# Output rows 0 to 3 projected in two parts, the sparse features before the differential ones

## The chip, the core and the metric

The kernel runs on one core of a Trainium2 chip. The core has five engines with an instruction stream each: TensorE (PE in the profile; its weight loads are PEld), VectorE (DVE), ScalarE (ACT), GpSimd (POOL) and SyncE (SP), which issues nearly all transfers here. An engine takes its instructions in order and waits on semaphores for the others. The metric is the device time of one execution in microseconds (us).

## The reference

One decoder layer on 1024 tokens of width 1024, in float32. `h = x @ w_in` gives queries, keys, values and gates. Two groups of heads share it. The differential group (4 heads of 128 features) computes two causal softmaxes per head, subtracts one from the other, multiplies by the values and normalizes each row. The sparse group (8 heads of 64) adds a compressed, a selected and a window attention. Then:

```python
mix = jnp.concatenate([o_diff, o_nsa], axis=-1) @ w_out[l]
x = layer_norm(DEEPNORM_ALPHA * x + mix, ln1_g[l], ln1_b[l])
ffn = (jax.nn.silu(x @ w_gate[l]) * (x @ w_up[l])) @ w_down[l]
x = layer_norm(DEEPNORM_ALPHA * x + ffn, ln2_g[l], ln2_b[l])
```

So 512 of the 1024 features that `w_out` multiplies are differential (k = 0 to 3 in pieces of 128, one piece a head) and 512 are sparse (k = 4 to 7).

## The kernel before

The 1024 tokens are 8 rows of 128. A product in near float32 is made of three matmuls (`mm3`, L116 to L118): each operand is split into a high part, a cast on ScalarE (L81), and a low part, a subtraction on VectorE or GpSimd (L83); high x high, high x low and low x high are summed in one bank of PSUM. There are eight banks: two named psS (scores), three psT (transposes), one psO (attention times values) and two psM (projections).

Attention goes by units. A unit of a differential head is one row of 128 queries. Its front half makes the scores (L323, L326) in pieces of up to 512 keys, adds distances and takes the minimum on VectorE (L332), and takes the exponentials on ScalarE (L346); its back half transposes the weights (L355) and multiplies by the values (L481). When four rows of a head are through (rows 0 to 3 or 4 to 7), `finish` normalizes them (L495 on VectorE, L496 on GpSimd, L497 on VectorE), transposes them (L500, the tile `od`), scales them on ScalarE (L503) and stores them to DRAM, into `mix_d` (L505). The sparse heads store theirs there too, all of them before the last four phases.

What happens between the units is set by a table, `phases`. A row of it names units and a list of fillers: generators that issue the projections of the next heads, and at the end the output projection. A function `pump` draws from the list at a rate that the fillers' stated costs and the units' costs give, and gives what it draws a lower priority. The final order on each engine is then made by a scheduler from these priorities; the order listings below show what it made.

The output projection of row i (`out_fill` for rows 0 to 3, `out_start` and `out_half_now` for rows 4 to 7): x of the row is loaded to `acc[i]`, the mixed features of the row are loaded from `mix_d` into two `w` tiles of which there are five (the sparse half first, then the differential), and for each half of the output's columns 8 pieces k, in the order 4 to 7 and then 0 to 3, are summed in one bank; then `acc = ALPHA * acc + bank` on VectorE (L605). The `w_out` weights lie in eight tiles of the pool `big`, which has eight; they replace the tiles of `x` (four for tokens 0 to 511, four for 512 to 1023) once no projection reads these. `norm1` is the layer norm of a row (L633, L645 to L648, L655) and its store. After the attention, `x_put` transposes the normalized rows (L913) and `x_sums` forms sums of rows i and i-4 (L929 to L934) for the gate and up products, whose first matmul reads `x11h`.

A row's differential half has all four differential heads in it, so its load waits until head 3's half (rows 0 to 3, or 4 to 7) is stored.

Of the kernel before, what the change touches and what calls it, by code (L numbers as in the profile page):

```python
# [17 lines left out]
P = 128  # L18
# [19 lines left out]
def layer_kernel(ctx: ExitStack, tc: tile.TileContext, xT, x, w_t, w_vg, w_dv, lam_in, subln,  # L38
# [21 lines left out]
    def ps_m():  # L60
        return psum.tile([P, 512], F32, tag="M", name="psM", bufs=2)
# [31 lines left out]

    def load_split_here(src, hi, lo, l_eng="dve", order=(0,)):

        n = 1024 // len(order)
        for k in order:
            raw = lo[:, k * n:(k + 1) * n].bitcast(F32)
            nc.sync.dma_start(raw, src[:, k * n:(k + 1) * n])
            split(raw, hi[:, k * n:(k + 1) * n], lo[:, k * n:(k + 1) * n], l_eng)  # L100
        return hi, lo

    def w_tiles():
        lo = w_tile()
        return w_tile(), lo
# [4 lines left out]
    def big_tiles():  # L110
        t = big_tile()
        return [t[:, 0, :], t[:, 1, :]]

    def mm3(acc, ah, al, bh, bl, first, last, more=False):

        nc.tensor.matmul(acc, lhsT=ah, rhs=bh, start=first, stop=False, skip_group_check=more)  # L116
        nc.tensor.matmul(acc, lhsT=ah, rhs=bl, start=False, stop=False, skip_group_check=more)  # L117
        nc.tensor.matmul(acc, lhsT=al, rhs=bh, start=False, stop=last, skip_group_check=more)  # L118
# [25 lines left out]
    with ExitStack() as ctx_a:  # L144
# [294 lines left out]

            return [make(i, kind) for i in range(NB) for kind in range(2)]  # L440

        late = []

        def diff_units(h, qt, kd, V):
            slope = SLOPES[h]
# [2 lines left out]
            def make(i):  # L448
# [42 lines left out]
                def finish(orow, ss, r0):  # L491

                    nc.vector.tensor_mul(r0, r0, r0)
                    nc.vector.tensor_scalar(r0, r0, EPS, None, op0=ALU.mult)
                    nc.vector.scalar_tensor_tensor(ss, ss, 1.0 / P, r0, op0=ALU.mult, op1=ALU.add)  # L495
                    nc.gpsimd.tensor_tensor(ss, ss, mhalf[:, :4], op=ALU.pow)  # L496
                    nc.vector.tensor_mul(orow, orow, ss.unsqueeze(2).to_broadcast([P, 4, P]))  # L497
                    tp = ps_t()
                    for n in range(4):
                        nc.tensor.transpose(tp[:, n * P:(n + 1) * P], orow[:, n, :], ident)  # L500
                    for n in range(2):
                        md = small([P, 256], "tmp", 3)
                        nc.scalar.activation(md, tp[:, n * 256:(n + 1) * 256], AF.Copy, scale=g08)  # L503
                        b = hf * 4 + n * 2
                        nc.sync.dma_start(mix_d[b:b + 2, :, h, :].rearrange("i p t -> p i t"),  # L505
                                          md.rearrange("p (i t) -> p i t", t=P))

                return front, back, 2.0 * (i + 1) + 1

# [67 lines left out]
                    yield 0.0  # L577
            return steps, 0.0

        def wo_fill(nh):  # L580
            def steps():
                for kp in range(KT // 2):
                    wo[nh, kp] = load_split_here(wo_d[nh, kp], *big_tiles(), l_eng="pool", order=(0, 1))
                yield 0.0
            return steps, 0.0

        mix_rows = {}

        def out_start(i):

            acc[i] = slot((8, 9, 10, 11, 4, 2, 3, 5)[i], F32)
            nc.sync.dma_start(acc[i], x[i * P:(i + 1) * P, :])
            mix_rows[i] = load_split_here(mix_d[i].rearrange("p k t -> p (k t)"), *w_tiles(),
                                           "dve" if i < 4 else "pool", order=(1, 0))

        def out_half(i, nh, ps):
            m = mix_rows[i]
            cs = slice(nh * 512, (nh + 1) * 512)
            for k in (4, 5, 6, 7, 0, 1, 2, 3):
                ks = slice(k * P, (k + 1) * P)  # L600
                ws = slice((k % 2) * 512, (k % 2 + 1) * 512)
                w = wo[nh, k // 2]
                mm3(ps, m[0][:, ks], m[1][:, ks], w[0][:, ws], w[1][:, ws], k == 4, k == 3)
                yield 0.65
            nc.vector.scalar_tensor_tensor(acc[i][:, cs], acc[i][:, cs], ALPHA, ps, op0=ALU.mult, op1=ALU.add)  # L605

        def norm1(i, **kw):
            layer_norm(acc[i], **kw)
            nc.sync.dma_start(x1_d[i], acc[i])

        def out_fill(i, normed):
            def steps():
                out_start(i)
                for nh in range(2):
                    yield from out_half(i, nh, ps_m())
                if normed:
                    norm1(i)
            return steps, 10.4

        def norm_params(src, after=None):  # L620
            lnp[:] = [slot(0, F32), slot(1, F32)]
# [156 lines left out]
        def qdf(h, hf, tiles=w_tiles):  # L778
            return q_fill(8 + 2 * h, hf, qd[h], tiles)
# [14 lines left out]
        def held_fill():  # L794

            def steps():
# [23 lines left out]
            ([(diff, 2, range(4))],  # L820
             [kdf(3, 0), kdf(3, 1), qdf(3, 0)], 2, 1.25, 130, None),
            ([(diff, 3, range(4))],
             [qdf(2, 1), dvf(1, range(4, 8))], 2, 1.25, 60, None),
            ([(diff, 2, (4, 7, 6, 5))],
             [wo_fill(0), qdf(3, 1), wo_fill(1), held_fill(), out_fill(0, False), out_fill(1, False)], 2, 1.25, 40, None),
            ([(diff, 3, range(4, 8))],
             [ln_fill((0, 1)), out_fill(2, True), out_fill(3, True)], 2, 0.9, 60, None),
        ]
        pending = []

# [103 lines left out]
        nc.gpsimd.tensor_sub(b21, b21, t2)  # L934

    def out_half_now(i, nh, ps):
        for _ in out_half(i, nh, ps):
            pass

    for i in (4, 5):  # L940
        out_start(i)
# [329 lines left out]
```

## Time and profile before

| what | us |
| --- | --- |
| median of 3 runs (lowest, highest) | 1305.22 (1305.02, 1305.49) |
| the profiled execution, its time | 1305.84 |
| its span, first to last instruction | 1304.1 |
| TensorE busy | 1286.2 (99%) |
| VectorE busy | 917.8 (70%) |
| ScalarE busy | 652.1 (50%) |
| GpSimd busy | 464.1 (36%) |
| mean granted TensorE clock | 0.999 |

A row of the timeline gives the start and the duration in us, the engine, the line of the kernel, the operation, out<-in with the tiles' names, the shape and how many; behind it, in brackets, the engine's idle time before it and what ended it. A matmul's duration overlaps the next one's, so how long one takes in a stream is read from start to start.

### The profile page before, as it was taken

Reading aid. Unit: us, or ns where it says so; the run is one execution under the profiler, and the core shown is the slowest. Engines: PE = TensorE matmul, PEld = TensorE weight load, DVE = VectorE, ACT = ScalarE, POOL = GpSimd, SP = SyncE. Lnnn points to the kernel's source line nnn. Section 1 sums busy time; section 2 is a strip of 40 time slices with the busy share of each in tenths; the row PEclk is TensorE's granted clock in tenths of the full one; section 3 lists DMA queues with packets and bytes.
Section 4 is the critical chain, followed back from the end, with each engine's and each line's share of the span. In section 5 each row is a group of like instructions: output and inputs, shape, how many; then the busy total and the mean of one; then the engine's idle time right before and its main releaser. Section 6 shows DMA issues by size and latency. Waiting matters only on the chain.

```text
span 1304.1 us, 20490 instructions
## 1 busy us (share of the span) xinstructions
PE 1286.2 (99%) x6955; PEld 1107.8 (85%) x6955; DVE 917.8 (70%) x1963; ACT 652.1 (50%) x1398; POOL 464.1 (36%) x499
## 2 busy tenths in 40 slices
PE   9999999999999999999999999999999999999997
PEld 7998999988988889788887888888888888888886
DVE  5567867778778667774797677776766768555588
ACT  5366866868776566653353333333333335533330
POOL 4434534545435446643613313232231222000071
PEclk9999999999999999999999999999999999999999
DMA  9412012121112135623224566555555559768641
GB/s 354 132 31 62 22 35 62 49 48 48 35 55 70 50 94 149 218 82 113 81 76 149 180 232 228 194 178 173 174 170 185 187 179 346 259 200 291 195 168 65
DMA packets 86841, 183.13 MB, mean 140 GB/s; under 512 B 10576, under 2 KB 19152, under 8 KB 86608
## 3 DMA queue, kind: packets, MB, share of 16 engines
q1 hardware_dynamic: 86736, 181.82, 42.7%
q8 instruction: 55, 0.90, 0.3%
q14 instruction: 50, 0.41, 0.1%
HBM read 116.18 MB, written 57.15 MB: 133 GB/s over the span
## 4 chain that ended last, share of the span: by engine, by line
PE 91%; DVE 4%; DMA 2%; ACT 2%; issue 1%; POOL 0%; SPq 0%; DVEq 0%; ACTq 0%
PE psM L116 11%; PE psM L118 11%; PE psM L117 11%; PE psS L118 6%; PE psS L117 6%; PE psS L116 6%; PE psT L118 5%; PE psT L117 5%; PE psT L116 5%; PE psT L365 4%; PE psS L323 3%; PE psS L326 3%; PE psO L428 2%; PE psO L426 2%; PE psO L481 2%; PE psO L116 2%
## 5 line engine op out<-in xcount | busy, mean ns | idle before, releaser
L346 ACT ACTIVATE t<-t,m 128x384 f32<-128x384 f32 (+7 forms) x192 | 144.2, 752 | 65.4 <-DVE m L332 59.8
L411 POOL TENSOR_SCALAR t<-t,r,gates 128x640 f32<-128x640 f32 (+7 forms) x128 | 99.6, 783 | 180.5 <-DVE r L405 82.4
L116 PE MATMUL psM<-big,w 128*128 128x512 f32 x304 | 120.6, 397 | 0.6 <-DVE slot L171 0.3
L118 PE MATMUL psM<-big,w 128*128 128x512 f32 x304 | 120.1, 396 | 0.0
L117 PE MATMUL psM<-big,w 128*128 128x512 f32 x304 | 119.9, 394 | 0.0
L323 PE MATMUL psS<-slot,q 128*128 128x320 f32 (+10 forms) x304 | 111.8, 369 | 2.2 <-DVE m L332 2.0
L1019 POOL TENSOR_TENSOR half<-half,half 128x512 f32<-128x512 f32 x22 | 33.5, 1524 | 205.0 <-ACT half L1018 205.0
L83 DVE TENSOR_TENSOR pt<-psT,pt 128x512 fp32r<-128x512 f32 (+1 forms) x152 | 91.3, 615 | 13.1 <-ACT pt L81 11.7
L326 PE MATMUL psS<-slot,q 128*128 128x320 f32 (+10 forms) x304 | 99.5, 329 | 0.0
L81 ACT CAST pt<-psT 128x512 fp32r<-128x512 f32 (+1 forms) x152 | 77.3, 525 | 20.6 <-PE psT L365 10.0
L81 ACT CAST big<-slot 128x1024 fp32r<-128x1024 f32 (+1 forms) x54 | 54.4, 1018 | 66.2 <-DVE slot L1011 50.5
L83 DVE TENSOR_TENSOR op<-op 128x1024 fp32r<-128x1024 f32 x44 | 60.9, 1388 | 36.3 <-ACT op L81 35.8
L83 DVE TENSOR_TENSOR big<-slot,big 128x1024 fp32r<-128x1024 f32 (+1 forms) x54 | 63.5, 1182 | 30.5 <-ACT big L81 30.3
L365 PE MATMUL psT<-ident,t 128*128 128x128 f32 x528 | 83.8, 273 | 0.8 <-DVE pt L83 0.7
L81 ACT CAST op<-op 128x1024 fp32r<-128x1024 f32 x44 | 45.9, 1052 | 61.8 <-DMA op<-t_d 55.6
L428 PE MATMUL psO<-pt,slot 128*128 128x256 f32 x264 | 72.1, 294 | 0.1
L426 PE MATMUL psO<-pt,slot 128*128 128x256 f32 x264 | 71.8, 289 | 0.0
L332 DVE CUSTOM_DVE_ANT_0 t<-psS,dsel 128x384 f32<-128x384 f32 (+9 forms) x128 | 62.3, 493 | 13.4 <-PE psS L326 9.6
L1023 POOL TENSOR_TENSOR half<-half,half 128x512 f32<-128x512 f32 x22 | 36.5, 1659 | 99.0 <-DVE half L1022 98.8
L81 ACT CAST big<-big 128x1024 fp32r<-128x1024 f32 (+1 forms) x49 | 44.2, 912 | 45.6 <-DMA big<-t_d 34.0
L118 PEld LDWEIGHTS psM<-big,w 128*128 128x128 f32 x304 | 57.1, 188 | 11.4
L116 PEld LDWEIGHTS psM<-big,w 128*128 128x128 f32 x304 | 57.2, 188 | 11.1 <-ACT w L81 0.8
(371 smaller groups left out, 3971.3 us busy)
## 6 DMA issues: line engine op xcount, KB each, us to landing
a_d<-slot SPq DMA_DIRECT2D x77, 256.0 KB, 3.0
t_d<-slot SPq DMA_DIRECT2D x77, 256.0 KB, 2.2
q<-q SPq DMA_DIRECT2D x48, 256.0 KB, 2.9
slot<-in_w_up_dram SPq DMA_DIRECT2D x22, 512.0 KB, 3.8
slot<-in_w_down_dram SPq DMA_DIRECT2D x22, 512.0 KB, 3.9
op<-a_d SPq DMA_DIRECT2D x44, 256.0 KB, 3.5
op<-t_d SPq DMA_DIRECT2D x44, 256.0 KB, 4.0
big<-a_d SPq DMA_DIRECT2D x33, 256.0 KB, 2.9
```

Of the source, the lines that this page charges most:

```text
L81: nc.scalar.copy(hi, src)
L83: eng.tensor_sub(lo, src, hi.bitcast(F32))
L116: nc.tensor.matmul(acc, lhsT=ah, rhs=bh, start=first, stop=False, skip_group_check=more)
L117: nc.tensor.matmul(acc, lhsT=ah, rhs=bl, start=False, stop=False, skip_group_check=more)
L118: nc.tensor.matmul(acc, lhsT=al, rhs=bh, start=False, stop=last, skip_group_check=more)
L323: mm = nc.tensor.matmul(ps[:, :c + part], lhsT=q[0], rhs=k[:, ks], start=True, stop=False)
L326: nc.tensor.matmul(ps[:, :c + part], lhsT=q[1], rhs=k[:, ks], start=False, stop=True)
L346: nc.scalar.activation(t[:, :width], t[:, :width], AF.Exp, bias=m, scale=-1.0, accum_out=r)
L365: nc.tensor.transpose(tp[:rows, n * P:(n + 1) * P], s, ident)
L411: nc.gpsimd.tensor_scalar(t, t, r[:, c:c + 1], gates[:, i, gc:gc + 1], op0=ALU.mult, op1=ALU.mult)
L426: nc.tensor.matmul(po[:, :256], lhsT=v, rhs=pt[:, 0, n * 256:(n + 1) * 256], start=False, stop=False)
L428: nc.tensor.matmul(po[:, :256], lhsT=v, rhs=pt[:, 1, n * 256:(n + 1) * 256], start=False, stop=last)
```

## The change

Rows 0 to 3 of the output are projected in two parts. A part is half of the features (four pieces k) for both halves of the columns; it loads its half of the mixed row into one `w` tile, high and low beside each other, and is put down by itself. The sparse part (part 1) loads x of the row and does `acc = ALPHA * acc + bank`; the differential part (part 0) does `acc = acc + bank`. The sparse parts of rows 0 to 3 stand as fillers from the phase of head 3's rows 0 to 3 on; the differential parts behind `held_fill` and in the last phase. The weights are loaded for the sparse pieces of both column halves first (`wo_fill((2, 3))`), and for the differential ones later. Rows 4 to 7 keep their form.

```diff
-        def wo_fill(nh):
+        def wo_fill(kps):
             def steps():
-                for kp in range(KT // 2):
-                    wo[nh, kp] = load_split_here(wo_d[nh, kp], *big_tiles(), l_eng="pool", order=(0, 1))
+                for nh in range(2):
+                    for kp in kps:
+                        wo[nh, kp] = load_split_here(wo_d[nh, kp], *big_tiles(), l_eng="pool", order=(0, 1))
...
+        def out_mm(nh, ps, m, ks, k, first, last):
+            w, ws = wo[nh, k // 2], slice((k % 2) * 512, (k % 2 + 1) * 512)
+            mm3(ps, m[0][:, ks], m[1][:, ks], w[0][:, ws], w[1][:, ws], first, last)
...
-        def out_fill(i, normed):
+        def out_fill(i, part, normed=False):
             def steps():
-                out_start(i)
+                if part:
+                    row_start(i)
+                t = w_tile()
+                m = t[:, 0:512], t[:, 512:1024]
+                src = mix_d[i].rearrange("p k t -> p (k t)") if part else mix_row(i)
+                load_split_here(src[:, part * 512:(part + 1) * 512], *m, "dve")
                 for nh in range(2):
-                    yield from out_half(i, nh, ps_m())
+                    ps, cs = ps_m(), slice(nh * 512, (nh + 1) * 512)
+                    for k in range(4):
+                        out_mm(nh, ps, m, slice(k * P, (k + 1) * P), 4 * part + k, k == 0, k == 3)
+                        yield 0.65
+                    if part:
+                        nc.vector.scalar_tensor_tensor(acc[i][:, cs], acc[i][:, cs], ALPHA, ps,
+                                                       op0=ALU.mult, op1=ALU.add)
+                    else:
+                        nc.vector.tensor_add(acc[i][:, cs], acc[i][:, cs], ps)
                 if normed:
                     norm1(i)
-            return steps, 10.4
+            return steps, 5.2
...
             ([(diff, 3, range(4))],
-             [qdf(2, 1), dvf(1, range(4, 8))], 2, 1.25, 60, None),
+             [wo_fill((2, 3)), qdf(2, 1), dvf(1, range(4, 8)), out_fill(0, 1)], 2, 1.25, 60, None),
             ([(diff, 2, (4, 7, 6, 5))],
-             [wo_fill(0), qdf(3, 1), wo_fill(1), held_fill(), out_fill(0, False), out_fill(1, False)], 2, 1.25, 40, None),
+             [out_fill(1, 1), qdf(3, 1), wo_fill((0, 1)), out_fill(2, 1), out_fill(3, 1), held_fill(), out_fill(0, 0)],
+             2, 1.25, 40, None),
             ([(diff, 3, range(4, 8))],
-             [ln_fill((0, 1)), out_fill(2, True), out_fill(3, True)], 2, 0.9, 60, None),
+             [ln_fill((0,)), out_fill(1, 0, True), out_fill(2, 0, True), out_fill(3, 0, True)], 2, 0.9, 60, None),
```

The new functions `row_start` (the load of x) and `mix_row` (the row in DRAM) are pieces of the old `out_start`. In the listings line numbers of the change are higher by some 20 than the same line's before: L913 and L935 are the transposes of `x_put`, L605 and L613 the old addition of a half row, L648 and L669 the last addition of a layer norm, L929 and L951 the first of `x_sums`.

First place: TensorE, shortly ahead of the transposes of head 3's first half (`od_6708`), while head 2's last scores (128x384) and products with the values (psO) are made. Before:

```order
L326 MATMUL psS_7178<-slot0_6049,q_6786 128x384
L481 MATMUL psO_6973<-slot6_5637,pt_6979 128x128 x4
L323 MATMUL psS_7183<-slot1_6050,q_6787 128x384
L326 MATMUL psS_7183<-slot1_6050,q_6787 128x384
L323 MATMUL psS_7188<-slot1_6050,q_6787 128x384
L326 MATMUL psS_7188<-slot1_6050,q_6787 128x384
L481 MATMUL psO_7019<-slot6_5637,pt_7025 128x128 x4
L323 MATMUL psS_7327<-slot2_6467,q_7084 128x320
```

And with the change:

```order
L117 MATMUL psM_7303<-big_6723,w_7299 128x512
L481 MATMUL psO_7035<-slot6_5637,pt_7041 128x128 x4
L323 MATMUL psS_7181<-slot1_6050,q_6770 128x384
L326 MATMUL psS_7181<-slot1_6050,q_6770 128x384
L323 MATMUL psS_7186<-slot1_6050,q_6770 128x384
L326 MATMUL psS_7186<-slot1_6050,q_6770 128x384
L118 MATMUL psM_7303<-big_6723,w_7299 128x512
L116 MATMUL psM_7317<-big_6730,w_7299 128x512
```

The rows psM belong to the sparse part of row 3 (`w_7299`, weights `big`); twelve of psM_7317 follow before the next L481, where before no projection stood. From the transposes of head 2's first half to these of head 3's, 72 matmuls with 512 columns of projection and output stand now, 18 before.

Second place: TensorE at the transposes of head 3's second half. Before (`od_7456`; psM_7683 is row 3's second half of the columns, of which 22 matmuls and three more groups of transposes follow until psS_7857, row 4's first differential piece):

```order
L117 MATMUL psM_7683<-big_7105,w_7647 128x512
L500 MATMUL psT_7776<-ident_74,od_7456 128x128 x4
L913 MATMUL psT_7815<-ident_74,slot8_7135 128x128 x4
L913 MATMUL psT_7822<-ident_74,slot8_7135 128x128 x4
L118 MATMUL psM_7683<-big_7105,w_7646 128x512
L116 MATMUL psM_7683<-big_7105,w_7647 128x512
```

And with the change (psS_7873 and psS_7899 are row 4's two banks, `w_7814` the high part of its mixed row):

```order
L118 MATMUL psM_7981<-big_6737,w_7823 128x512
L500 MATMUL psT_7792<-ident_74,od_7500 128x128 x4
L935 MATMUL psT_7831<-ident_74,slot8_6929 128x128 x4
L935 MATMUL psT_7838<-ident_74,slot8_6929 128x128 x4
L935 MATMUL psT_7845<-ident_74,slot9_7093 128x128 x4
L935 MATMUL psT_7852<-ident_74,slot9_7093 128x128 x4
L935 MATMUL psT_7859<-ident_74,slot10_7252 128x128 x4
L116 MATMUL psS_7873<-big_7224,w_7814 128x512
L117 MATMUL psS_7873<-big_7224,w_7814 128x512
```

The transposes of rows 0 to 2 now stand together between head 3's transposes and row 4's first differential piece, and no output matmul with them.

Third place: VectorE at row 6 (`slot3`) and row 7 (`slot5`). Before:

```order
L648 TENSOR_TENSOR slot3_8023<-slot3_8023,slot1_7471 128x1024
L929 TENSOR_TENSOR slot10_7498<-slot3_8023,slot10_7498 128x512
L930 TENSOR_TENSOR half0_8179<-slot3_8023 128x512
L932 TENSOR_TENSOR half1_8180<-slot3_8023,slot10_7498 128x512
L605 SCALAR_TENSOR_TENSOR slot5_8033<-slot5_8033,psM_8153 128x512
L655 BN_STATS st_8199<-slot5_8033 128x6
L633 BN_AGGR mv_8202<-st_8199 128x2
```

And with the change:

```order
L613 SCALAR_TENSOR_TENSOR slot5_8049<-slot5_8049,psM_8169 128x512
L676 BN_STATS st_8215<-slot5_8049 128x6
L669 TENSOR_TENSOR slot3_8039<-slot3_8039,slot1_7515 128x1024
L654 BN_AGGR mv_8218<-st_8215 128x2
L951 TENSOR_TENSOR slot10_7252<-slot3_8039,slot10_7252 128x512
L952 TENSOR_TENSOR half0_8195<-slot3_8039 128x512
L129 TENSOR_SCALAR mv_8218<-mv_8218 128x1
L659 SCALAR_TENSOR_TENSOR slot5_8049<-slot5_8049,mv_8218,slot0_7514 128x512 x2
L954 TENSOR_TENSOR half1_8196<-slot3_8039,slot10_7252 128x512
```

The end of row 6's norm and its two differences (`half0`, `half1`, which TensorE transposes next) stand behind row 7's last half row instead of ahead of it.

More of the change, by code (lines that the diff above doesn't have):

```diff
@@ L94, in load_split_here @@
     def load_split_here(src, hi, lo, l_eng="dve", order=(0,)):
-        n = 1024 // len(order)
+        n = src.shape[-1] // len(order)
         for k in order:
@@ L440, in nsa_units @@
             return [make(i, kind) for i in range(NB) for kind in range(2)]
-        late = []
+        late, mixed = [], set()
         def diff_units(h, qt, kd, V):
@@ L506, in finish @@
                                           md.rearrange("p (i t) -> p i t", t=P))
+                    mixed.add((h, hf))
                 return front, back, 2.0 * (i + 1) + 1
@@ L587, in layer_kernel, with row_start, mix_row, out_start @@
         mix_rows = {}
-        def out_start(i):
+        def row_start(i):
             acc[i] = slot((8, 9, 10, 11, 4, 2, 3, 5)[i], F32)
             nc.sync.dma_start(acc[i], x[i * P:(i + 1) * P, :])
-            mix_rows[i] = load_split_here(mix_d[i].rearrange("p k t -> p (k t)"), *w_tiles(),
-                                           "dve" if i < 4 else "pool", order=(1, 0))
+        def mix_row(i):
+            assert all((h, i // 4) in mixed for h in range(4))
+            return mix_d[i].rearrange("p k t -> p (k t)")
+        def out_start(i):
+            row_start(i)
+            mix_rows[i] = load_split_here(mix_row(i), *w_tiles(), "pool", order=(1, 0))
+        def out_mm(nh, ps, m, ks, k, first, last):
+            w, ws = wo[nh, k // 2], slice((k % 2) * 512, (k % 2 + 1) * 512)
+            mm3(ps, m[0][:, ks], m[1][:, ks], w[0][:, ws], w[1][:, ws], first, last)
         def out_half(i, nh, ps):
-            m = mix_rows[i]
             cs = slice(nh * 512, (nh + 1) * 512)
             for k in (4, 5, 6, 7, 0, 1, 2, 3):
[L600 to L604, printed above, removed]
+                out_mm(nh, ps, mix_rows[i], slice(k * P, (k + 1) * P), k, k == 4, k == 3)
             nc.vector.scalar_tensor_tensor(acc[i][:, cs], acc[i][:, cs], ALPHA, ps, op0=ALU.mult, op1=ALU.add)
@@ L609, in norm1 @@
             nc.sync.dma_start(x1_d[i], acc[i])
-        def out_fill(i, normed):
+        def out_fill(i, part, normed=False):
             def steps():
-                out_start(i)
-                for nh in range(2):
-                    yield from out_half(i, nh, ps_m())
+                if part:
+                    row_start(i)
+                t = w_tile()
+                m = t[:, 0:512], t[:, 512:1024]
+                src = mix_d[i].rearrange("p k t -> p (k t)") if part else mix_row(i)
+                load_split_here(src[:, part * 512:(part + 1) * 512], *m, "dve")
+                for nh in range(2):
+                    ps, cs = ps_m(), slice(nh * 512, (nh + 1) * 512)
[7 more added lines that the diff above has]
+                        nc.vector.tensor_add(acc[i][:, cs], acc[i][:, cs], ps)
                 if normed:
                     norm1(i)
-            return steps, 10.4
+            return steps, 5.2
         def norm_params(src, after=None):
@@ L936, in out_half_now @@
     def out_half_now(i, nh, ps):
-        for _ in out_half(i, nh, ps):
-            pass
+        out_half(i, nh, ps)
     for i in (4, 5):
```

## The prediction, made before the change was run

> **What bounds the kernel now.** I read the page first, then the busy time by stage, then TensorE's instructions in order of time around the rows the change moves, and last the waits.
>
> ```profile
> span 1304.1 us, 20490 instructions
> PE 1286.2 (99%) x6955; PEld 1107.8 (85%) x6955; DVE 917.8 (70%) x1963; ACT 652.1 (50%) x1398; POOL 464.1 (36%) x499
> ```
>
> TensorE is busy for 99% of the span, and the change takes no matmul away and adds none: the output projection of rows 0 to 3 stays 4 x 2 x 8 x 3 matmuls. So the change can only win time in which TensorE stands still, and lose by making it stand still elsewhere. The stages say where it stands:
>
> ```profile
> 530.00:550.00 20.00, 17.49 (x109) 14.36 (x107) 17.41 (x50) 16.03 (x39) 16.43 (x15) 1.00 0.56 166
> 550.00:670.00 120.00, 119.77 (x630) 101.47 (x629) 81.43 (x147) 46.60 (x91) 54.23 (x44) 1.00 0.28 95
> 670.00:690.00 20.00, 19.03 (x108) 15.58 (x107) 18.68 (x30) 13.26 (x25) 3.44 (x2) 1.00 0.21 67
> ```
>
> The columns are the stretch, its length, and the busy time of PE, PEld, DVE, ACT, POOL. Between 550 and 670 us, where all remaining projection work of rows 0 to 7 lies today, TensorE lacks 0.23 us. Between 530 and 550 it lacks 2.51 us, with VectorE at 17.41 of 20. That hole is what the change can fill: heads 2 and 3 are being scored there, VectorE and ScalarE work at their limit, and row 0's two half rows have used up the output work that does not need head 3. Its five largest gaps:
>
> ```profile
> 532.45 0.39 PE L326 MATMUL psS<-slot,q 128*128 128x512 f32 x1
> 533.21 0.50 PE L323 MATMUL psS<-slot,q 128*128 128x512 f32 x1 [0.37 <-DVE m L332]
> 538.23 0.37 PE L326 MATMUL psS<-slot,q 128*128 128x448 f32 x1
> 538.71 0.94 PE L481 MATMUL psO<-slot,pt 128*128 128x128 f32 x6
> 541.18 0.34 PE L326 MATMUL psS<-slot,q 128*128 128x384 f32 x1
> 541.77 1.16 PE L481 MATMUL psO<-slot,pt 128*128 128x128 f32 x8 [0.25 <-ACT ms L486]
> 543.12 0.34 PE L323 MATMUL psS<-slot,q 128*128 128x384 f32 x1
> 543.30 0.34 PE L326 MATMUL psS<-slot,q 128*128 128x384 f32 x1
> 544.25 1.16 PE L481 MATMUL psO<-slot,pt 128*128 128x128 f32 x8 [0.61 <-ACT ms L486]
> 545.68 0.31 PE L326 MATMUL psS<-slot,q 128*128 128x320 f32 x1
> 547.07 0.63 PE L500 MATMUL psT<-ident,od 128*128 128x128 f32 x4 [1.08 <-DVE r L463]
> ...
> 660.02 0.39 PE L117 MATMUL psS<-x11l,big 128*128 128x512 f32 x1
> 660.25 0.39 PE L118 MATMUL psS<-x11h,big 128*128 128x512 f32 x1
> ```
>
> A row's duration overlaps the next row, so a gap is counted from start to start, less what the first one needs: 0.23 us for 512 columns (660.02 to 660.25), 0.18 for 384 (543.12 to 543.30), and in proportion 0.21 for 448 and 0.15 for 320. That gives 0.53 + 0.27 + 0.41 + 0.77 + 1.24 = 3.2 us.
>
> **Term 1, the hole is filled.** In the new order 72 matmuls of projection and output stand between the transposes of head 2's and head 3's first halves, where 18 stood (first pair of order listings); at 0.23 us that is 12 us more for VectorE and ScalarE to keep up. I take 3.5 us: the five gaps and a little for the small ones. Bounds 2.5 (the idle time of the window alone) and 4.5, if the wait behind head 3's transposes shrinks too. The copies of weights, the loads of x and of the mixed rows keep their number; eight additions on VectorE at 0.68 us are new (5.4 us), and so are narrower waits on a bank, all where VectorE has 81 of 120 us; without that cover they would cost up to 5.4 us. On SP's queue the copies of head 3's second query now stand behind eight weight loads and a load of the norm's scale:
>
> ```profile
> q<-q SPq DMA_DIRECT2D x48, 256.0 KB, 2.9
> ```
>
> Two in series are 5.8 us; 48 output matmuls, 11 us, stand between that projection and the first score on it. I cost it at nothing; with 3 us more in the queue and the copy on VectorE late it would begin to show.
>
> **Term 2, the round trip of head 3 is uncovered.** Rows 4 to 7 still wait for head 3's second half: transposes of its rows, scaling on ScalarE, a store to DRAM, a load back, a cast, and then the first matmul of row 4's differential half.
>
> ```profile
> 609.41 0.60 PE L500 MATMUL psT<-ident,od 128*128 128x128 f32 x4
> 609.85 1.04 PE L913 MATMUL psT<-ident,slot 128*128 128x128 f32 x8
> 610.64 0.48 PE L118 MATMUL psM<-big,w 128*128 128x512 f32 x1
> ...
> 617.00 0.48 PE L116 MATMUL psS<-big,w 128*128 128x512 f32 x1
> ```
> ```profile
> 610.05 0.84 ACT L503 ACTIVATE tmp<-psT,g 128x256 f32<-128x256 f32 x2 [8.58 <-PE psT L500]
> ...
> 615.35 0.62 ACT L81 CAST w<-w 128x512 fp32r<-128x512 f32 x1 [3.35 <-DMA w<-mix_d]
> ```
> ```profile
> 610.55 0.89 SPq L505 DMA_DIRECT2D mix_d<-tmp  x2
> 612.52 11.54 SPq L99 DMA_DIRECT2D w<-mix_d  x6
> ```
>
> From the transposes at 609.41 to the end of the cast at 615.97 it is 6.56 us. Today row 3's last 22 matmuls cover it, and TensorE starts row 4 at 617.00 without waiting. In the new order row 3 is finished by then, and only 24 transposes stand in between (second pair of listings): 12 of them took 1.23 us (609.41 to 610.64), so 24 take 2.5, and TensorE waits 4.1 us. It can't fetch other work: it takes its instructions in order. Bounds: 3.5 if the extra transposes are held up by their three banks and fill part of the wait, 5 if the two loads of gate and up weights ahead of the store in SP's queue still move when it is issued.
>
> **Term 3, the way to those transposes.** Behind the last product of head 3 now come 12 matmuls (2.7 us) and then the transposes. The chain they wait for:
>
> ```profile
> 598.73 1.95 PE L481 MATMUL psO<-slot,pt 128*128 128x128 f32 x16
> ```
> ```profile
> 600.72 0.29 DVE L485 COPY od<-psO 128x128 f32<-128x128 f32 x1 [1.41 <-PE psO L481]
> 601.50 1.58 DVE L495 SCALAR_TENSOR_TENSOR ss<-ss,r 128x4 f32<-128x4 f32 x1 [0.49 <-ACT ms L486]
> 605.24 0.69 DVE L497 TENSOR_TENSOR od<-od,ss 128x512 f32<-128x512 f32 x1 [0.91 <-POOL ss L496]
> ```
>
> From 600.68 to 605.93 it is 5.3 us today, with a GpSimd multiplication and a VectorE addition of row 2 in the middle; after the earlier half of head 3 it was 547.07 - 542.93 = 4.1. Of the 2.7 us, 2.5 lie behind the end of the product's row. Wait: 1.6 to 2.8 as measured; with neither engine held up perhaps 0.5 less than the shorter. In the new order row 2 is through and row 3's multiplication comes behind the chain, so I take 1.0; bounds 0.5 and 2.8.
>
> **Term 4, the last rows on VectorE.** From head 3's last transposes to the first gate product stand 196 instructions of TensorE where 242 stood, at 0.23 us some 11 us less (done earlier instead), while rows 4 to 7 still need the same normalizations and sums on VectorE. The third pair of listings shows the effect: row 6's normalized sum now stands behind row 7's last half row.
>
> ```profile
> 656.39 1.21 DVE L648 TENSOR_TENSOR slot<-slot,slot 128x1024 f32<-128x1024 f32 x1
> 657.64 0.69 DVE L929 TENSOR_TENSOR slot<-slot,slot 128x512 f32<-128x512 f32 x1
> 659.45 0.68 DVE L605 SCALAR_TENSOR_TENSOR slot<-slot,psM 128x512 f32<-128x512 f32 x1
> 660.16 0.69 DVE L655 BATCH_NORM_STATS2 st<-slot 128x6 f32<-128x512 f32 x1
> 660.89 0.21 DVE L633 BATCH_NORM_AGGREGATE mv<-st 128x2 f32<-128x12 f32 x1
> 661.21 1.40 DVE L638 SCALAR_TENSOR_TENSOR slot<-slot,mv,slot 128x512 f32<-128x512 f32 x2
> ```
>
> From row 7's half row to row 6's second difference VectorE works 0.68 + 0.69 + 1.21 + 0.21 + 3 x 0.69 + 1.40, and a tenth for a small one: 6.4 us. TensorE has 24 matmuls and four transposes for it, 24 x 0.23 + 0.4 = 5.9, and some 0.3 passes before VectorE starts. Wait 0.8 us; bounds 0 and 2.7 (VectorE up to 2 us behind by then).
>
> **Sum.** -3.5 + 4.1 + 1.0 + 0.8 = +2.4 us. The profiled execution had a span of 1304.1 and a time of 1305.84, so 1.7 lie around the span; the new span is 1306.5, its time 1308.2. The median of the runs, 1305.22, is 0.6 below the profiled one: 1307.6 us, 0.18% more. About 0.2%, 2.6 us, is what a measurement here tells from no change.
>
> [...] The longest wait of TensorE in the trace is short, and half speed is seen only at the start, where 16 matmuls took 5.80 - 2.36 = 3.44 us, 0.215 each; a transpose of that size takes 1.23 / 12 = 0.10 later.
>
> ```profile
> 2.36 3.79 PE L674 MATMUL psO<-ident 128*128 128x128 f32 x16 [2.36 <-POOL ident masks.py:199]
> 5.80 0.77 PE L116 MATMUL psS<-big,w 128*128 128x512 f32 x1
> ```
>
> [...]
>
> **The rivals.** (a) The clock falls in the new wait of 4.1 us: for the stretch that the start needed at half speed, at least 3.4 us, half the work is lost, 2 us more: 1309.6. [...] (b) VectorE becomes the bound of rows 4 to 7: term 4 at 2.7 and term 3 at 2.8, 3.7 us more: 1311.3. It decides once VectorE is over 1 us behind TensorE at row 7. For it: 18.68 of 20 us busy right after, at 670; against it: the slack of 550 to 670. (c) The other side, faster: TensorE already stood behind head 3's first half too (547.07, then row 0's differential half), and 0.97 us are idle at 670 to 690. If term 1 gives 4.5, the rows normalized earlier free 1 us there, and terms 2 to 4 come to 3 us, it ends at -2.5 to -3: 1302.5. For it: rows 1 to 3 are normalized sooner; against it: the round trip has no shorter path. (d) It does not do what it says: attention still runs dry, because its own chain on VectorE sets the pace with fillers or without, and no new wait appears: 1305.2.
>
> **Chances.** The forecast 50%, with its own range 1305.5 to 1309.5; (a) 8%, (b) 20%, (c) 14%, (d) 8%. Of the forecast's half a quarter lies above 1307.8, so slower is 0.08 + 0.20 + 0.13 = 0.41, faster is (c) at 0.13, the rest, 0.46, is no change that can be measured. The range 1303.0 to 1311.0 leaves out most of (c) and the far part of (b).
>
> **What would show it.** Step 1: between the transposes of heads 2 and 3 no TensorE gap over 0.5 us. Step 2: a wait of TensorE near 4 us at the first matmul of row 4's differential half, ended by a cast or its load; this is the step on which the sign hangs. If it is under 2 us I am wrong, and the kernel is faster. Step 3: the last transposes of head 3 wait about 1 us for VectorE's multiplication. Step 4: row 6's second difference is waited for, under 1 us. A granted clock below 1 behind the wait would show (a).

## The result, and the profile after

The changed kernel takes 1316.36 us (median of 4 runs, 1316.15 to 1317.11); the kernel before, run beside it, takes 1305.12. The ratio is 1.0086, with a 95% interval from 1.0072 to 1.0100: 11.2 us slower, where 2.4 were forecast and the range ended at 1311.0. The page of the changed kernel:

```profile
span 1314.7 us, 20503 instructions
PE 1290.3 (98%) x6955; PEld 1111.2 (85%) x6955; DVE 922.9 (70%) x1971; ACT 651.8 (50%) x1398; POOL 465.7 (35%) x499
PEclk9999999999999999999899999999999999999999
```

The profiled execution took 1316.48 us, and its span is 10.6 us longer than before. The matmuls are as many, 6955, but TensorE is *busy* 4.1 us longer: some of them ran slower. The clock row has one 8. The busy time by stage, first of the kernel before, then of the changed one (length; busy time and instructions of PE, PEld, DVE, ACT, POOL; granted clock; DMA share; GB/s):

```profile
530.00:560.00 30.00, 27.26 (x170) 22.74 (x167) 24.09 (x67) 21.75 (x54) 18.35 (x17) 1.00 0.46 139
...
610.00:640.00 30.00, 30.00 (x150) 25.12 (x148) 18.94 (x30) 11.33 (x19) 18.07 (x14) 1.00 0.33 114
...
670.00:710.00 40.00, 38.77 (x193) 31.59 (x192) 33.26 (x50) 21.55 (x39) 8.58 (x6) 1.00 0.28 93
```
```profile
530.00:560.00 30.00, 27.14 (x134) 22.71 (x133) 15.11 (x38) 14.19 (x35) 17.32 (x14) 0.94 0.41 123
...
610.00:640.00 30.00, 25.13 (x129) 20.54 (x128) 13.03 (x24) 9.67 (x20) 8.37 (x8) 0.89 0.36 124
...
670.00:710.00 40.00, 36.95 (x190) 29.68 (x189) 37.46 (x59) 22.16 (x41) 7.46 (x5) 1.00 0.27 99
```

TensorE loses time in three stages. In two of them the clock fell as well: 0.94 over 30 us is 3.4 us at half speed, and 0.89 is 6.8 us. Half of what TensorE works at half speed is lost beside the waits: 1.7 us of the first, and 2.9 us of the second, since TensorE still stands idle for 1.1 of the 6.8 us (row 626.99 further down). The idle time of TensorE went from 2.74 + 1.23 = 4.0 us to 2.86 + 4.87 + 3.05 = 10.8. Lost time counted as the prediction did, from start to start less what each shape needs, and summed over all rows of a stretch:

| stretch | before | after | of it, half clock | forecast | came |
|---|---|---|---|---|---|
| the hole, 530 to 560 | 4.9 | 5.0 | 1.7 | -3.5 | +0.1 |
| head 3's round trip, after 610 to 640 | 0.2 | 8.8 | 2.9 | +4.1 + 1.0 | +8.6 |
| last rows, before 670 to 700, after 670 to 710 | 2.6 | 4.9 | 0 | +0.8 | +2.3 |

With +0.2 from small gaps and -0.6 from before 500 us that is the 10.6 of the span.

**The hole is filled, and has a new one.** TensorE works without a gap up to 548 us and then stands:

```profile
547.81 0.34 PE L326 MATMUL psS<-slot,q 128*128 128x384 f32 x1
551.01 0.50 PE L116 MATMUL psM<-big,w 128*128 128x512 f32 x1 [2.86 <-DVE slot L633]
...
552.16 0.63 PE L117 MATMUL psM<-big,w 128*128 128x512 f32 x1
552.59 0.63 PE L118 MATMUL psM<-big,w 128*128 128x512 f32 x1
```

It waits for a bank, which VectorE's sum into an output row (L633) sets free. VectorE, ScalarE and GpSimd in this stretch:

```profile
543.76 0.08 DVE L332 DVE_READ_ACCUMULATOR2_ANT m<- 128x1 f32 x1
547.79 0.16 DVE L463 RECIPROCAL r<-r 128x1 f32<-128x1 f32 x1 [3.95 <-ACT t L346]
...
548.59 1.77 DVE L466 SCALAR_TENSOR_TENSOR t<-t,r 128x560 f32<-128x560 f32 x1
550.28 0.67 DVE L633 SCALAR_TENSOR_TENSOR slot<-slot,psM 128x512 f32<-128x512 f32 x1
```
```profile
542.82 1.65 ACT L81 CAST big<-big 128x512 fp32r<-128x512 f32 x3
...
545.10 0.62 ACT L81 CAST big<-big 128x512 fp32r<-128x512 f32 x1
...
546.10 0.63 ACT L81 CAST big<-big 128x512 fp32r<-128x512 f32 x1
546.62 1.05 ACT L346 ACTIVATE t<-t,m 128x896 f32<-128x896 f32 x1
```
```profile
543.50 6.25 POOL L83 TENSOR_TENSOR big<-big 128x512 fp32r<-128x512 f32 x5 [0.26 <-ACT big L81]
```

The exponential at 546.62 had its minimum at 543.84. Ahead of it on ScalarE stand five casts of the second part of the output weights, which had just landed. VectorE waits 3.95 us for the exponential, and the sum that would free the bank stands behind VectorE's softmax work. That work is slower as well: L464 takes 0.56 us and L466 1.77, beside GpSimd's subtractions for the same weights. Ahead of them, at 536.10 us of this trace, L464 takes 0.22 us, and in experiment 2 the L466 of this size takes 0.80. By these rows some 1.3 of the 2.86 us (an estimate) come from GpSimd's part of the burst, the rest from ScalarE's. Behind the wait a 512-column matmul starts every 0.43 us, not every 0.23: half clock.

**The round trip.** TensorE, then the cast it waits for, the load ahead of that cast, and VectorE:

```profile
619.97 0.63 PE L500 MATMUL psT<-ident,od 128*128 128x128 f32 x4 [0.19 <-DVE od L497]
620.44 1.75 PE L935 MATMUL psT<-ident,slot 128*128 128x128 f32 x12
623.95 1.26 PE L935 MATMUL psT<-ident,slot 128*128 128x128 f32 x8 [1.77 <-DVE x11l L83]
628.07 0.79 PE L116 MATMUL psS<-big,w 128*128 128x512 f32 x1 [2.86 <-ACT w L81]
```
```profile
627.40 0.62 ACT L81 CAST w<-w 128x512 fp32r<-128x512 f32 x1 [4.33 <-DMA w<-mix_d]
```
```profile
623.11 1.28 SPq L99 DMA_DIRECT2D w<-mix_d  x3
```
```profile
622.07 1.23 DVE L669 TENSOR_TENSOR slot<-slot,slot 128x1024 f32<-128x1024 f32 x1 [2.25 <-POOL slot L668]
623.21 0.68 DVE L83 TENSOR_TENSOR x11l<-psT,x11h 128x512 fp32r<-128x512 f32 x1
```

From the transposes at 619.97 to the end of the cast at 628.02 the round trip takes 8.05 us, 1.5 more than before. The 1.5 us come in the load of the mixed row: from its issue to the cast it is 4.29 us (623.11 to 627.40), and 2.83 before (612.52 to 615.35). Three such loads and the store of a row go out within 1.4 us here; whether they hold one another up was not tested. The waits are 0.19 + 1.77 + 2.86 = 4.8 us. The middle one is VectorE's queue: the copies that free the transposes' banks stand behind row 3's norm, whose addition (L669) waits for GpSimd's multiplication.

**The last rows.** TensorE waits for row 6's second difference, as term 4 had it:

```profile
674.56 0.63 PE L935 MATMUL psT<-ident,half 128*128 128x128 f32 x4 [1.36 <-DVE half L954]
```

**The clock.** The half-speed stretches of this trace begin at 551.89 and 626.99 us. They are 75.1 us apart and last 3.41 and 6.83 us; 75.1 us are 22 stretches of 3.41. Cut on that grid (columns as above):

```profile
548.48:551.89 3.41, 0.88 (x4) 0.75 (x5) 3.37 (x6) 1.09 (x4) 3.41 (x4) 1.00 0.48 154
551.89:555.31 3.42, 3.42 (x10) 2.64 (x9) 1.02 (x4) 1.35 (x4) 2.80 (x3) 0.50 0.73 153
...
620.16:623.57 3.41, 1.97 (x16) 1.50 (x14) 1.50 (x2) 2.40 (x5) 1.88 (x1) 1.00 0.40 132
623.57:626.99 3.42, 1.26 (x8) 0.84 (x8) 1.52 (x3) 0.00 (x0) 0.00 (x0) 1.00 0.69 198
626.99:630.40 3.41, 2.33 (x7) 1.84 (x8) 1.38 (x2) 2.11 (x4) 2.31 (x2) 0.50 0.46 186
630.40:633.81 3.41, 3.41 (x11) 2.73 (x10) 0.69 (x1) 0.59 (x1) 0.21 (x1) 0.50 0.00 0
633.81:637.23 3.42, 3.42 (x16) 2.81 (x15) 1.39 (x2) 0.00 (x0) 0.00 (x0) 1.00 0.00 0
```

Each row is followed by a clock that fits how much TensorE worked in it: after 0.88 and 1.26 us of work the next stretch runs at half, after 1.97 it does not; a half-speed stretch with 2.33 is followed by another, a full one (630.40) by full speed. By these rows it isn't the length of a wait that counts, but how much TensorE works in a stretch of 3.41 us. Waits of no more than 2.86 us were enough here. At the end of the kernel the clock falls once more, at 1309.65 us, 682.66 us behind 626.99, which is 200 stretches of 3.413.

### The profile page after: what moved, and what is told of

It reads as the page before. It is cut to its first block, busy times and chain, and to the rows that moved or that the text cites. A ratio compares the mean times of both kernels' runs of the same rounds, so it can differ in the third digit from the quotient of the medians.

```text
span 1314.7 us, 20503 instructions
## 1 busy us (share of the span) xinstructions
PE 1290.3 (98%) x6955; PEld 1111.2 (85%) x6955; DVE 922.9 (70%) x1971; ACT 651.8 (50%) x1398; POOL 465.7 (35%) x499
## 4 chain that ended last, share of the span: by engine, by line
PE 89%; DVE 4%; issue 2%; ACT 2%; POOL 1%; DMA 1%; DVEq 0%; SPq 0%; ACTq 0%; POOLq 0%
PE psM L116 10%; PE psM L118 10%; PE psM L117 10%; PE psT L116 5%; PE psT L117 5%; PE psT L118 5%; PE psS L118 5%; PE psS L117 5%; PE psS L116 5%; PE psT L365 4%; PE psS L323 3%; PE psS L326 3%; PE psO L428 2%; PE psO L481 2%; PE psO L426 2%
```

## The experiments

Line numbers in the rows are each kernel's own. The kernel before, run beside them, took 1304.9 to 1305.3 us.

**1. Work in the round trip's wait.** Matmuls that nobody reads, and in a second kernel transposes, behind row 1's transposes:

```diff
     for i in range(4):
         x_put("11", i, acc[i][:, LO])
         x_put("21", i, acc[i][:, HI])
+        if i == 1:
+            dum, behind = ps_o(), x_tr[-1]
+            with tc.issue_after(behind):
+                for _ in range(14):
+                    nc.tensor.matmul(dum, lhsT=wo[0, 2][0][:, 0:P], rhs=wo[0, 2][0][:, 0:512], start=True, stop=True)
```

> The changed kernel with 14 matmuls of 512 columns, whose result nobody reads, put between the transposes of row 1 and those of row 2, that is into the wait of 2.86 us that the changed kernel has there (14 x 0.23 = 3.2 us). The output is the same; the only thing that is added is that TensorE works in the wait. Theory A (the clock): after this wait the changed kernel's granted clock is one half for 6.83 us, which costs 3.4 us; with work in the wait it stays at 1.00, and the kernel takes 1316.4 - 3.4 = 1313.0 us, with the casts that end the wait at the same place. Rival B (the slow matmuls behind the wait are slow because their loads and casts are late, and the clock record goes along with it): the added 3.2 us only take the place of the wait, and the time stays at 1316.4 us or grows by some tenths.

> The same place filled with 29 transposes of 128 x 128 (29 x 0.109 = 3.2 us) in place of the 14 matmuls, so TensorE is as busy by its rows as with the matmuls. Theory A1 (any work keeps the clock): the time of the kernel with matmuls in the wait, 1313.0 us by theory A, granted clock 1.00. Theory A2 (transposes are not counted as work, so a stretch of some 7 us that holds transposes alone lets the clock fall): the clock falls as in the changed kernel, and the time is 1316.4 us or up to 1.7 us more, since the transposes themselves then run at half speed in part. [...]

Measured: 1314.39 us with matmuls (1311.81 to 1315.90; ratio to the kernel before 1.0069, 1.0054 to 1.0084) and 1313.52 with transposes (1312.18 to 1315.30; 1.0065, 1.0050 to 1.0080). Both are better than 1316.4, but neither reaches 1313.0, and their runs spread over 3 to 4 us, with mean clocks from 0.995 to 0.999. The grid rows, of the kernel with transposes:

```profile
620.56:623.97 3.41, 1.59 (x13) 1.11 (x11) 1.86 (x3) 2.40 (x5) 1.51 (x1) 1.00 0.34 109
623.97:627.39 3.42, 3.40 (x16) 3.41 (x17) 1.16 (x2) 0.27 (x1) 0.00 (x0) 0.50 0.82 261
627.39:630.80 3.41, 3.41 (x30) 3.31 (x29) 0.95 (x2) 2.24 (x5) 2.52 (x2) 1.00 0.30 123
```

The clock fell before the added work began, through the *first* wait (1.77 us), so the experiment was half a test. It did settle the transposes: in the stretch from 623.97 to 627.39 TensorE does nothing but transpose (16 instructions in 3.40 us, which the trace lists as matmuls), and the clock is back at 1.00 behind it. Theory A2 falls.

**2. Casts spread.** The second part of the weights is listed later, and two casts, with their loads and GpSimd's subtractions, are tied behind each of four exponentials:

```diff
-             [out_fill(1, 1), qdf(3, 1), wo_fill((0, 1)), out_fill(2, 1), out_fill(3, 1), held_fill(), out_fill(0, 0)],
+             [out_fill(1, 1), qdf(3, 1), out_fill(2, 1), wo_fill((0,), (-4, -3)), out_fill(3, 1), wo_fill((1,), (-2, -1)), held_fill(), out_fill(0, 0)],
...
+                        with tc.issue_after(exp_at[behind[nh]]) if behind else ExitStack():
```

> The changed kernel with the second part of the output weights (the eight casts on ScalarE and eight subtractions on GpSimd) listed later and tied so that only two casts stand behind each exponential of head 2's last two units, where six stood ahead of one of them. Theory C: the first long wait of the changed kernel (2.86 us, ended at 551.0 us by VectorE's sum into a row) comes from ScalarE's casts ahead of an exponential that was ready at 543.8 us and ran at 546.6; then the wait shrinks under 0.5 us, the clock does not fall at 551.9 us, and the kernel takes 1316.4 - 2.9 - 1.7 = 1311.8 us. Rival D (attention's own chain over VectorE and GpSimd sets the pace there, casts or no casts): a wait of 2 to 3 us stays, the clock falls, 1316 us. Rival E (the casts are only in another's way): the wait moves to the units of head 3 behind, and half is won, 1314 us.

Measured: 1310.68 us (1309.27 to 1310.81; 1.0038, 1.0024 to 1.0053), 5.7 less than the change. The stage has no idle time and no half clock left:

```profile
530.00:560.00 30.00, 30.00 (x168) 26.02 (x167) 19.26 (x50) 17.21 (x43) 20.29 (x17) 1.00 0.46 141
```

VectorE's L466, which took 1.77 us in the change, is short again:

```profile
545.79 0.80 DVE L466 SCALAR_TENSOR_TENSOR t<-t,r 128x560 f32<-128x560 f32 x1
```

Theory C holds for the changed kernel: with the fillers in place, the burst of the second weights made the wait. The edit moves casts and subtractions alike, so it doesn't part ScalarE's share from GpSimd's.

**3. Row 3's differential part and row 5's sparse part late, besides.** The 24 matmuls of row 3 behind head 3's last product, the 24 of row 5 behind head 3's last transposes (`behind` holds the instruction that the matmuls of `out_mm` are tied to):

```diff
-             [ln_fill((0,)), out_fill(1, 0, True), out_fill(2, 0, True), out_fill(3, 0, True)], 2, 0.9, 60, None),
+             [ln_fill((0,)), out_fill(1, 0, True), out_fill(2, 0, True)], 2, 0.9, 60, None),
...
+        behind.append(od_pv[-1])
+        for _ in out_fill(3, 0, True)[0]():
+            pass
+        behind.clear()
...
+    behind.append(od_tr[-1])
     for nh in range(2):
         out_half_now(5, nh, ps_m())
+    behind.clear()
```

> The casts spread as before, and besides the 24 matmuls of row 3's differential part queued behind head 3's last product (they then cover the normalization ahead of the transposes), and row 5's sparse part, 24 matmuls, behind head 3's last transposes (they cover the round trip). Theory A + C: neither long wait is left, and the clock stays at 1.00: 1316.4 - 4.6 for the first wait - 2.9 - 1.8 - 3.4 for the second, 1303.7 us, if the attention of head 3's last two units, which loses 48 matmuls of cover, doesn't run dry; with 1 to 3 us of gaps there 1305 to 1307. Rival F (VectorE's work on the last rows is the bound, so that what is won before it is lost at rows 6 and 7): the waits move to the first products of the feed-forward part, and the time is 1308 us or more.

> The changed kernel with row 3's differential part behind head 3's last product and row 5's sparse part behind its last transposes, the weights' casts where the change has them. Theory A (what was lost at the round trip, 8.8 us with the clock, goes, and 3 us of new gaps come where the 48 matmuls stood, as in the kernel with both edits): 1316.4 - 8.8 + 3 = 1310.6 us, with the first wait and, where the windows fall so, its half clock still there. Rival (the two edits only work together, since the casts' lateness carries over to head 3): 1313 us or more.

Measured: 1305.77 us with both edits (1305.08 to 1308.71; 1.0007, 0.9998 to 1.0017), 1311.10 with this one alone (1310.89 to 1312.93; 1.0050, 1.0035 to 1.0066). The two edits add up, as theory A says: 5.7 and 5.3 us alone, 10.6 together. No wait is left at the round trip. One of the new gaps, in the kernel with both edits, by TensorE and VectorE:

```profile
605.45 2.05 PE L481 MATMUL psO<-slot,pt 128*128 128x128 f32 x16 [1.72 <-ACT ms L487]
```
```profile
603.57 1.23 DVE L672 TENSOR_TENSOR slot<-slot,slot 128x1024 f32<-128x1024 f32 x1 [3.91 <-POOL slot L671]
604.71 0.28 DVE L486 COPY od<-psO 128x128 f32<-128x128 f32 x1
```

Head 3's last product waits for a bank. The bank is free when VectorE has copied it (L486) and ScalarE has read it behind that (L487). The copy is short, but it stands on VectorE behind the norm's addition (L672), and that waits for GpSimd. It is the pattern of the 1.77 us above.

**4. The other half of the change alone.** The kernel before with the sparse features' weights first and casts spread, rows undivided:

```diff
-             [qdf(2, 1), dvf(1, range(4, 8))], 2, 1.25, 60, None),
+             [wo_fill((2, 3)), qdf(2, 1), dvf(1, range(4, 8))], 2, 1.25, 60, None),
...
-             [wo_fill(0), qdf(3, 1), wo_fill(1), held_fill(), out_fill(0, False), out_fill(1, False)], 2, 1.25, 40, None),
+             [qdf(3, 1), wo_fill((0,), (-4, -3)), wo_fill((1,), (-2, -1)), held_fill(), out_fill(0, False), out_fill(1, False)], 2, 1.25, 40, None),
```

> The kernel before with the other half of the change alone: the sparse features' output weights loaded first for both halves, the other weights' casts two behind each exponential of head 2's last units; the rows 0 to 3 are projected undivided as before. Theory D (the hole of the kernel before between 530 and 560 us, 4.9 us of lost time by the starts, is there because the two half rows that fit the free banks are used up and TensorE has nothing to fetch): the hole stays, 1305 us, or 1307 if it is long enough in one piece to let the clock fall. Theory C (the hole is made by the weights' casts and subtractions ahead of head 2's exponentials and products): it shrinks to 1 us or less, 1301 to 1302 us.

Measured: 1312.67 us (1312.23 to 1313.53; 1.0061, 1.0047 to 1.0074). Its stage, and two rows of the grid:

```profile
530.00:560.00 30.00, 24.37 (x121) 20.31 (x120) 19.44 (x54) 19.19 (x47) 20.02 (x17) 0.77 0.40 120
...
541.56:544.97 3.41, 2.21 (x9) 1.25 (x10) 3.19 (x10) 2.84 (x7) 3.41 (x3) 1.00 0.33 114
544.97:548.38 3.41, 2.57 (x13) 2.27 (x12) 2.14 (x6) 0.88 (x4) 3.41 (x4) 0.50 0.52 193
```

The hole is deeper: 5.6 us idle, and 0.77 over 30 us is 13.8 us at half clock. The hole stays though the casts are spread, so C falls here. D has the side right, but its time, 1305 or 1307 us, is missed by 5.7 us or more. The edit also takes fillers away: between the transposes of heads 2 and 3 stand 12 matmuls of 512 columns here, and 18 in the kernel before. So the run shows that TensorE runs dry where fillers are lacking, casts spread or not; what the casts alone cost the kernel before it doesn't show. With experiment 2, where divided rows leave no idle time in the stretch, it bears out the prediction's reading of the hole (no fillers).

**5. VectorE's queue: the norm's addition on GpSimd.**

```diff
-            layer_norm(acc[i], **kw)
+            layer_norm(acc[i], add_on=nc.gpsimd if i < 6 else nc.vector, **kw)
...
-            nc.vector.tensor_add(y, y, lnp[1])
+            add_on.tensor_add(y, y, lnp[1])
```

> The kernel with the casts spread and row 3 late, and besides the norm's last step of rows 0 to 5, the addition of the shift (1.23 us on VectorE), on GpSimd. In the run without it TensorE waits 1.72 us at 603.7 us: the last product needs its bank, which VectorE copies only behind such an addition, which in turn waits for GpSimd's multiplication; and it waits 1.36 us at 663.3 us for VectorE's differences of row 6. Theory G (VectorE's own queue is what both wait for): the first wait goes, the second falls by some 1 us, and the time falls from 1305.8 to 1303 us, below the kernel before. Rival H (row 6's chain of normalization sets the second wait, and GpSimd's addition, 2.4 us, is late for the next row): only the first goes, and 1 us is lost again: 1305 us.

> The kernel before with the same addition of rows 0 to 5 on GpSimd, nothing else. It has 2.6 us of lost time at the first products of the feed-forward part (670 to 700 us). Theory G (VectorE's queue): 1 us less, 1304 us. Rival H: no change, 1305 us.

> The changed kernel with the same addition on GpSimd, nothing else. Theory G: the 4.9 us lost at 670 to 710 us fall by 1 to 2, and the wait of 1.8 us of row 1's transposes, whose evacuation stands behind the addition of row 3 on VectorE, goes; but what it frees is lost again at the first product behind it, since that waits for the round trip: 1316.4 - 1.5 = 1315 us. If the wait in front of that product so becomes one piece of over 4 us, the clock falls as it does now. Rival H: 1316.4 us.

Measured: on top of experiment 3, 1304.50 us (1303.18 to 1304.99; 0.9993, 0.9985 to 1.0002); on the kernel before, 1305.15 (1.0003, 0.9994 to 1.0012), no change; on the changed kernel, 1313.37 (1311.96 to 1316.87; 1.0069, 1.0055 to 1.0083). On top of experiment 3 the wait ahead of head 3's last product went from 1.72 us to 0.39, and is no longer one for the bank but for the transposed weights (L358); the wait at the last rows stayed, now through GpSimd's queue (GpSimd, then TensorE):

```profile
647.50 3.35 POOL L672 TENSOR_TENSOR slot<-slot,slot 128x1024 f32<-128x1024 f32 x1
650.81 0.57 POOL L130 TENSOR_TENSOR mv<-mv,mhalf 128x1 f32<-128x1 f32 x1
```
```profile
663.10 0.63 PE L942 MATMUL psT<-ident,half 128*128 128x128 f32 x4 [1.30 <-DVE half L961]
```

Row 5's addition holds up row 6's power step (L130). So G holds for the first wait and H for the second.

The changed kernel with this edit gives the best view of the clock. Its first wait is 2.6 us long, nearly as in the change, and the clock does not fall: in this execution the wait lies across two stretches, with 2.31 and 1.93 us of work left in them:

```profile
546.72:550.14 3.42, 2.31 (x15) 1.83 (x13) 1.69 (x3) 3.40 (x8) 3.42 (x3) 1.00 0.32 114
550.14:553.55 3.41, 1.93 (x8) 1.61 (x9) 3.27 (x7) 0.37 (x2) 3.41 (x4) 1.00 0.46 162
```

This execution took 1311.96 us, the others of the same kernel 1313.3 to 1316.9, at mean clocks of 0.995 and 0.996 where it had 0.998. So much of what this kernel gains over the change can be the grid's luck, and its time says little about G; the wait of row 1's transposes did go from 1.77 to 0.7 us.

**6. The addition of row 5 back on VectorE** (`i < 5` in place of `i < 6`).

> As the kernel with the casts spread, row 3 late and the shift of rows 0 to 5 on GpSimd (1304.5 us), but the addition of row 5 back on VectorE. In that run row 5's addition on GpSimd (647.50 to 650.85 us) stood ahead of row 6's power step on the same engine (650.81), though row 6's variance was there at 644.97; row 6 was normalized late and TensorE waited 1.30 us for its second difference at 663.1. Theory G2 (the shift on GpSimd helps where GpSimd has nothing urgent behind it, and costs at row 5): the wait goes, and the time falls by 1.3 us, to 1303.2 us. Rival I (the tail is bound by row 7's own normalization, which comes next): the wait moves to row 7's differences, and the time stays at 1304.5 us.

Measured: 1303.77 us (1303.40 to 1304.76) beside 1305.12 for the kernel before; 0.9990, 0.9982 to 0.9999. This is the fastest version, and the interval just leaves out no change. The wait for row 6's second difference is gone. 0.7 us came and not 1.3, which the two intervals (0.9985 to 1.0002 without this edit) don't part from noise; a wait moved to row 7, as rival I has it. The longest wait of TensorE between 500 and 720 us is now:

```profile
PE psT L942 <- DVE xT3l L83: 0.9, 1, 0.9
```

**7. Work in both waits of the round trip**, the test that experiment 1 missed: on the kernel of experiment 2, seven of the idle matmuls behind row 1's first transposes, and seven behind its last.

> The kernel with the casts spread, 1310.7 us, and in it two times seven matmuls whose result nobody reads: behind the first four transposes of row 1, where it waits 1.77 us, and behind the last four, where it waits 1.79 us (7 x 0.23 = 1.6 us each, so neither wait is filled over). The first try, with all 14 in the second wait, was half a test: in its profile the clock had already fallen by 625.6 us, for the window of waits and transposes ahead of them. Theory A (the clock goes by how much TensorE works in each stretch of 3.41 us): with both waits filled no stretch is left empty, the granted clock stays at 1.00 in 600 to 640 us in every run, and the 6.83 us at half speed, 3.4 us, are won: 1310.7 - 3.4 = 1307.3 us. Rival B (the waits alone cost, the clock's fall costs nothing that the late loads wouldn't): 1310.7 us or more.

Measured: 1308.76 us (1308.04 to 1310.66; 1.0028, 1.0018 to 1.0038). The stage with the casts spread alone, and with work in both waits:

```profile
610.00:640.00 30.00, 26.20 (x126) 21.26 (x125) 15.20 (x27) 11.20 (x20) 12.42 (x11) 0.89 0.39 125
```
```profile
610.00:640.00 30.00, 29.29 (x153) 23.91 (x152) 16.59 (x28) 11.11 (x20) 14.16 (x13) 1.00 0.41 132
```

Matmuls without any use made the kernel 1.9 us faster by the medians, and the clock stays up; all nine runs have a mean clock of 0.998 or 0.999, the five without the work 0.996 to 0.998. The intervals of the two ratios (1.0024 to 1.0053 without the work) overlap, so the time alone leaves a doubt; the traces show the place. From head 3's transposes to the 13th matmul of 512 columns behind them, the added ones left out, it is 13.15 us without the work (starts 615.30 and 628.45) and 10.35 with it (616.38 and 626.73). Theory A holds, B falls. These 2.8 us are fewer than the 3.4 expected because TensorE stood idle in 0.75 of the 6.83 us at half speed, and half of the rest is 3.0. The two spans differ by 1.7 us only (1309.1 and 1307.4), so 1.1 is lost again elsewhere.

## Why the prediction was wrong

**The forecast lay on the right side, +2.4 us, and called it no change that can be measured; the kernel is 11.2 us slower.** By the prediction's own steps:

- **Term 1 (-3.5; came +0.1).** The fillers did close the five gaps (experiments 2 and 4). The step that failed is "The copies of weights, the loads of x and of the mixed rows keep their number": their number was kept, but not their place. The second part's casts now come in one burst among head 2's exponentials, and in ScalarE's queue they are ahead of them. That was costed at nothing with VectorE's 81 of 120 us as the cover. But those are the 120 us from 550 to 670, while the burst begins at 541; its work runs on ScalarE and GpSimd, and what it delays is a chain. It measured 2.9 us of wait and 1.7 of clock; spread, the casts cost nothing that shows.
- **Terms 2 and 3 (+4.1, +1.0; waits 0.2 + 1.8 + 2.9 = 4.8).** The sum was nearly right, in part by luck, since two errors met: the wait ahead of head 3's transposes is 0.2 and not 1.0, and the round trip is longer, 8.05 us against 6.56, by its load. Of the 4.1 us ahead of row 4's first product only 2.9 came there, since the transposes that were to cover 2.5 us of it were themselves held up for 1.8 us by VectorE's queue (bound 3.5 had named their banks).
- **The clock (rival (a), 8%, 2 us; came 2.9 us here, and 1.7 at term 1's wait).** This is the largest error. Two things failed: the chance, since the clock fell at waits of no more than 2.86 us, where (a) had one of 4.1; and the price, which took the half-speed stretch to be 3.4 us long, where it was 6.83. At the first wait, which no term had, the clock fell too, behind a stretch with 0.88 us of work. The whole of the 4.6 us is outside the forecast.
- **Term 4 (+0.8, bounds 0 and 2.7; came +2.3).** The mechanism was right and the size off: row 6's second difference is waited for, 1.36 us where less than 1 was said. Rival (b), which had this term at 2.7, is the nearest of the rivals by time, 1311.3, but it had the rest of its loss in term 3, at 2.8, where 0.2 came.
- **The chances.** The forecast's own range, 1305.5 to 1309.5, lies over 1307.8 by 1.7 of its 4 us, which is some 42% and not a quarter. With that, slower would have stood at 0.49, ahead of no change.

Without the two falls of the clock the hole would have come at -1.6 (3.3 against 4.9), the round trip at +5.7 and the last rows at +2.3; with the 0.2 and -0.6 that is +6.0 us, some 1311.2, at the edge of the range. The clock is the other 4.6.

## What to carry to other kernels

A transfer or a cast that "keeps its number" still has a place: before it is costed at nothing, look which chain is behind it in its engine's queue at the moment when its data land. Where TensorE is the bound, price a wait twice, as time and as clock: here a wait of 2.6 to 2.9 us cost 1.7 us more, or 2.9, or nothing, by where it fell; work in the gaps, matmuls that nobody reads, kept the clock up (1.00 from 610 to 640 us in experiment 7, 0.89 without). And an in-order engine that waits for another (here VectorE's addition for GpSimd's multiplication) passes its wait on to everything queued behind it. Moving the waiting instruction helped at one place (1.72 to 0.39 us) and was late for the next chain at another, so look what stands behind it on the new engine too.

## What the runs showed of the hardware that was not expected

In the changed kernel's trace the three falls of the clock lie on one grid of 3.413 us, 22 and 200 stretches apart, and the grid lies differently in other executions. Worked out from the starts of the falls (551.89 us here, 621.58 in experiment 2, 625.61 and 623.97 in experiment 1 with matmuls and with transposes), its first edge is some 2.3, 0.4, 1.0 and 2.7 us behind the span's start, an estimate. In the stretches that were read at full speed, the weight-load column gives this order: up to 1.11 us (experiment 1) they were followed by half speed, and from 1.50 us (620.16 in the changed kernel) on they were not. In between, two fell (1.16 at the end of the changed kernel, 1.25 in experiment 4) and two did not, 1.15 in the changed kernel itself and 1.21 in the kernel with row 3 late alone:

```profile
671.36:674.77 3.41, 1.82 (x11) 1.15 (x10) 3.41 (x7) 1.07 (x2) 1.26 (x2) 1.00 0.39 156
```
```profile
547.27:550.69 3.42, 1.53 (x11) 1.21 (x9) 2.25 (x3) 2.83 (x7) 3.42 (x4) 1.00 0.27 104
```

The matmul column draws no sharper line: 1.59 us (experiment 1) and 2.21 (experiment 4) fell, 1.53 and 1.82 did not. So neither column is quite what the clock goes by.

The way back took more: at half speed, stretches with 1.59 to 2.27 us of weight loads were followed by another, 2.57 (experiment 4) was too, 2.55 (the changed kernel in experiment 5) ended it, and so did 2.64 or more. One kernel's runs differ by up to 4.9 us (1311.96 to 1316.87, at mean clocks of 0.998 and 0.995) with nothing else changed: small gaps can cost more on one execution than on the next. What decides between 1.15 and 1.25 us is open.
